# Residual added to the blocks of an output product by accumulating transfers, and their squares queued behind a later weight cast

## The chip, the cores and the metric

The kernel runs on one core of a Trainium2 chip. The metric is device time in microseconds (us) of one execution; lower is better. Before the change it is 2038.79 us, the median of three runs (2037.45 to 2039.75). One execution was profiled, and all durations below come from it.

## The reference, cut to what matters

One layer of a block with 256 rows and a model width of 4096, all in float32:

```python
xn = rms_norm(h, norm_in_g)
q, k, v, z_a, a_c, g_c, z_c = split(xn @ w_in)            # 4096 x 14336
y_a = rms_norm(chunked_attention(q, k, v, rel_table), attn_out_g) * silu(z_a)
y_c = rms_norm(conv_module(a_c, g_c, ...), conv_out_g) * silu(z_c)
h = h + concatenate([y_a, y_c]) @ w_out                    # 4096 x 4096, the changed stage
gate = sigmoid(rms_norm(h, ple_norm_g) @ w_ple_gate + b)   # 4096 x 4096, the stage after it
h = h + gate * (p @ w_ple)
return rms_norm(h, final_g)
```

The change touches the line `h = h + ... @ w_out` (in the first term, `h` is the input `x`) and the sum of squares of its result, which the norm in the next line needs.

## The kernel before, in words

**Products.** Every float32 operand is split into a high part in the fp32r format and a remainder (`parts_of`, L199): ScalarE casts the weight tile `wt` into `wh` (L204), VectorE subtracts to make `wl` (L205). A product of two blocks is three matmuls: high by high, low by high, high by low. There are five `wt` buffers, filled by SyncE's DMAs (L403), and three each of `wh` and `wl`, so a cast waits until TensorE has finished with the tile three before it.

**Groups and pairs.** `mixed_product` (L327) makes one group: 1024 output columns (two column blocks j of 512) for both halves h of the rows, in four PSUM banks `acc[h][j]`. It walks over 16 pairs of contraction blocks. A plain pair takes 24 matmuls. A pair marked with a star takes seven products instead of eight, 21 matmuls, and needs sums of weights, `ua` and `ub`, which VectorE makes (L426 to L431) and which are cast and split too (`uh`, `ul`). Some of the seven go to four helper banks (`P1`, `P5`, `P6`, `P7`). After the group's last starred pair `on_helpers` empties these. The order of the pairs is written by hand: `dense` is "1 0* 3 2* 5 4* 6* 7 8* 9 10* 11 12* 14* 13 15", so two plain pairs follow the last starred one; `late` begins with eight plain pairs.

**The stage of the change** (L1044 to L1073) has four groups of `w_out`. For each, two tiles `hc` (128 partitions, 2 halves, 512 columns) are loaded from `x` (L1049). `on_helpers` (L1054) adds `P1` to the residual in place (L1057), makes three sums of helper banks in a scratch tile `z` (`helper_sums`, L464: a ScalarE copy at L467, four VectorE additions at L468 to L471), and folds these into `hc` with three more VectorE operations (L1059 to L1061). After the last pair VectorE adds the four banks `acc` (L1070), in the order (0,0), (1,0), (0,1), (1,1) of `QUARTERS`. For each quarter a square with a sum over the columns (`square_sum`, L498, run by ScalarE at L500) goes into the queue `later`, from which `fill` (L182) takes two entries after each pair. At the end the queue is emptied, and `rstd_of` (L502) makes the factor `r_h` from the sums (VectorE, then a power on GpSimd at L139).

**The stage after it**, four groups of `w_ple_gate` (L1082 and L1120 to L1164), uses the finished `hc` tiles as its left operand: `h_ahead` (L1037) has TensorE transpose them (L170), ScalarE make the high part (L156) and VectorE the remainder (L157), the first two tiles ahead of the last pair of the last `w_out` group and then one tile ahead of each second pair of the first gate group, whose order is `late` and whose `fill` takes four entries. `r_h` is first used in that group's `on_helpers`.

**Order on the engines.** A scheduler places the instructions at build time, by data and buffer dependences and by when it takes them to be ready. On the chip each engine's queue then runs strictly in that order: an instruction that waits holds everything behind it on its engine.

Of the kernel before, what the change touches and what calls it, by code (L numbers as in the profile page):

```python
# [3 lines left out]

# [6 lines left out]
F32 = mybir.dt.float32  # L11
F32R = mybir.dt.float32r
AF = mybir.ActivationFunctionType
ALU = mybir.AluOpType
AX = mybir.AxisListType

P = 128
NB = 512
# [7 lines left out]
def hybrid_block(  # L26
# [23 lines left out]
    nc = tc.nc  # L50
    _, T, D = x.shape
    NH = T // P
# [15 lines left out]
    def pool(name, bufs, stack=ctx, side=0, **kw):  # L68
        return stack.enter_context(tc.tile_pool(name=name, bufs=bufs, side=sides[side], **kw))

    cpool = pool("cpool", 1)
    act = pool("act", 8)
# [63 lines left out]
    def rsqrt(dst, src, n):  # L136

        nc.vector.tensor_scalar(dst, src, 1.0 / n, EPS, ALU.mult, ALU.add)
        nc.gpsimd.tensor_tensor(dst, dst, mhalf[:, : dst.shape[1]], ALU.pow)  # L139
# [40 lines left out]
    later = deque()  # L180

    def fill(n):  # L182
        for _ in range(min(n, len(later))):
            later.popleft()()


    def weight_parts(w, col, k0, kc, tiles=None):

        wt = wpool.tile([P, KC, NB], F32, tag="w", name="wt")
        nc.sync.dma_start(  # L190
            wt[:, :kc, :],
            w[k0 * P : (k0 + kc) * P, col : col + NB].rearrange("(k q) n -> q k n", q=P),
        )
        return parts_of(wt, kc, tiles)[0]

    def part_tiles():
        return [wpool.tile([P, KC, NB], F32R, tag=tag, name=tag, bufs=3) for tag in ("wh", "wl")]

    def parts_of(wt, kc, tiles=None):  # L199
        if tiles is None:  # L200
            tiles = part_tiles()
        wh, wl = tiles
        made = (
            nc.scalar.copy(wh[:, :kc, :], wt[:, :kc, :]),  # L204
            nc.vector.tensor_tensor(  # L205
                wl[:, :kc, :], wt[:, :kc, :], wh[:, :kc, :].bitcast(F32), ALU.subtract
            ),
        )
        return (wh, wl), made

    def accumulate(acc, h, lhs, kb, wh, wl, k, kblocks, then=lambda ins: None):
        t, i = lhs[kb // 4], kb % 4
        xh = t[:, i, 0, h * P : (h + 1) * P]
        xl = t[:, i, 1, h * P : (h + 1) * P]
        for kind in range(3):
            a, b = ((xh, wh), (xl, wh), (xh, wl))[kind]
            then(
                nc.tensor.matmul(  # L218
                    acc, a, b[:, k, :],
                    start=kb == 0 and kind == 0, stop=kb == kblocks - 1 and kind == 2,  # L220
                )
            )
# [85 lines left out]
    def pair_parts(src):  # L308

        tiles = [upool.tile([P, 2, NB], F32R, tag=tag, name=tag) for tag in ("uh", "ul")]  # L310
        return parts_of(src, 2, tiles)[0]
# [14 lines left out]

    def mixed_product(  # L327
        w, col, lhs, comb, order, on_helpers, ahead=None, fills=(0,), on_begin=None, apart=NB,
        left=(), begin=None,
    ):  # L330
# [64 lines left out]
        for n, (pair, seven) in enumerate(order):  # L395
# [9 lines left out]
            if n >= len(order) - n_left:  # L405
                for k in range(2):
                    tiles = left[2 * (n - len(order) + n_left) + k]
                    held.append((2 * pair + k, parts_of(wts[k], 2, tiles and tiles())[0]))
                fill(fills[n % len(fills)])
                continue  # L410
# [44 lines left out]
            if n == last_seven:  # L455
                on_helpers(helper)
# [4 lines left out]
    tt, stt = nc.vector.tensor_tensor, nc.vector.scalar_tensor_tensor  # L461
    QUARTERS = ((0, 0), (1, 0), (0, 1), (1, 1))

    def helper_sums(helper, z):  # L464


        nc.scalar.copy(z[1][0], helper["P1"])  # L467
        tt(z[1][0], helper["P6"], z[1][0], ALU.add)  # L468
        tt(z[0][1], helper["P5"], z[1][0], ALU.add)
        tt(z[1][0], helper["P7"], z[1][0], ALU.add)  # L470
        tt(z[1][1], helper["P5"], z[1][0], ALU.add)  # L471

    def sum_tiles():

        t = [spool.tile([P, NH, NB], F32, tag="stage", name="z") for _ in range(2)]
        return t, [[t[j][:, h] for j in range(2)] for h in range(NH)]

    def scaled_pair(w, col, apart, order, r, fills, **kw):

        t, z = [], []  # L480

        def on_helpers(helper):
            for dst, src in zip((t, z), sum_tiles()):
                dst.extend(src)
            nc.scalar.activation(z[0][0], helper["P1"], AF.Identity, scale=r[:, :1])
            helper_sums(helper, z)
            for h, j in QUARTERS[1:]:
                nc.scalar.activation(z[h][j], z[h][j], AF.Identity, scale=r[:, h : h + 1])

        c = mixed_product(w, col, xT, xS, order, on_helpers, fills=fills, apart=apart, **kw)  # L490
        for h, j in QUARTERS:
            stt(  # L492
                z[h][j], c[h][j], r[:, h : h + 1], z[h][j],
                ALU.mult, ALU.subtract if j else ALU.add,
            )
        return t

    def square_sum(dst, src, scale=1.0):  # L498
        junk = spool.tile([P, NB], mybir.dt.bfloat16, tag="junk", name="junk", bufs=1)
        return nc.scalar.activation(junk[:, : src.shape[1]], src, AF.Square, scale=scale, accum_out=dst)  # L500

    def rstd_of(partial, n, name):  # L502
        r = cpool.tile([P, partial.shape[1]], F32, name=name)
        nc.vector.tensor_reduce(r, partial, AX.X, ALU.add)
        rsqrt(r, r, n)
        return r
# [433 lines left out]
    for c0, order in zip(range(0, CW // NB, 2), point):  # L940
        row = broadcast_row(b_pw, c0 * NB, 2 * NB, tag="stage")
        rows = [row[:, j * NB : (j + 1) * NB] for j in range(2)]
        ys, z = [], []
# [4 lines left out]
        def on_helpers(helper):  # L948
            y_tiles()
            z.extend([ys[j][:, h, :] for j in range(2)] for h in range(NH))  # L950
            tt(z[0][0], helper["P1"], rows[0], ALU.add)
            helper_sums(helper, z)
            for h, j in QUARTERS[1:]:
                tt(z[h][j], z[h][j], rows[j], ALU.subtract if j else ALU.add)

        acc = mixed_product(w_pw[0], c0 * NB, uS, uC, order, on_helpers)
# [35 lines left out]
    def before_last(make):  # L992

        return lambda pair: make(0) if pair == dense[-1][0] else None
# [29 lines left out]
    hs, hT, hS = [], [], []  # L1024
# [17 lines left out]
                embedding()  # L1042

    ssq_h = cpool.tile([P, NH, D // NB], F32, name="ssq_h")  # L1044
    for c0 in range(0, D // NB, 2):
        for j in range(2):
            hc = act.tile([P, NH, NB], F32, tag="act", name="hc")
            c = c0 + j
            nc.sync.dma_start(  # L1049
                hc, x[0, :, c * NB : (c + 1) * NB].rearrange("(h q) n -> q h n", q=P)  # L1050
            )
            hs.append(hc)

        def on_helpers(helper):  # L1054
            _, z = sum_tiles()
            h00, h01, h10, h11 = (hs[c0 + j][:, h, :] for h in range(NH) for j in range(2))
            tt(h00, helper["P1"], h00, ALU.add)  # L1057
            helper_sums(helper, z)
            tt(h01, h01, z[0][1], ALU.subtract)  # L1059
            tt(h10, h10, z[1][0], ALU.add)  # L1060
            tt(h11, h11, z[1][1], ALU.subtract)  # L1061

        acc = mixed_product(
            w_out[0], c0 * NB, yT, yS, dense if c0 else late, on_helpers,
            ahead=y_ahead if c0 == 0 else before_last(h_ahead) if c0 + 2 == D // NB else None,
            fills=(2,),
        )
        for h, j in QUARTERS:
            hc = hs[c0 + j][:, h, :]
            tt(hc, acc[h][j], hc, ALU.add)  # L1070
            later.append(partial(square_sum, ssq_h[:, h, c0 + j : c0 + j + 1], hc))
    fill(len(later))
    r_h = rstd_of(ssq_h, D, "r_h")  # L1073


    n_f = D // NB
# [47 lines left out]
    c0 = n_f - 2  # L1124
    _, z = sum_tiles()
# [17 lines left out]
    def on_helpers(helper):  # L1143
# [4 lines left out]
    acc, add_left = mixed_product(  # L1148
        w_ple_gate[0], c0 * NB, hT, hS, final, on_helpers, fills=(4,), on_begin=on_begin,
        left=[None] * 3 + [kept] * 3,  # L1150
    )
# [119 lines left out]
```

## Time and profile before

| | us |
|---|---|
| median of 3 runs (lowest, highest) | 2038.79 (2037.45, 2039.75) |
| profiled execution | 2039.1 |
| its span in the profile | 2037.3 |
| TensorE busy in the span | 2019.6 |
| VectorE busy | 1887.9 |
| ScalarE busy | 1200.8 |
| GpSimd busy | 8.1 |
| the four `w_out` groups | about 1329 to 1664 of the span |
| first L1070 of each group | 1415.1, 1496.4, 1578.0, 1661.5 |

How to read it: times inside the execution are microseconds from the start of the span. A matmul's bar in the profile is 0.39 us long, but the next one begins about 0.227 us after it, so the bars overlap and a busy share of TensorE counts gaps only where they are longer than the overlap. "PE" is TensorE, "DVE" VectorE, "ACT" ScalarE, "POOL" GpSimd, "SP" SyncE (a q behind it is its queue).

### The profile page before, as it was taken

To read this page: it belongs to the slowest core of one execution; us is meant where nothing else is said; L and a number is where in the kernel's file an instruction comes from. 1 tells how busy PE (TensorE), PEld (TensorE's weight loads), DVE (VectorE), ACT (ScalarE), POOL (GpSimd) and SP (SyncE) were. 2 spreads that over 40 slices of the span, in tenths; PEclk is the share of its full clock that TensorE was granted. 3 is DMA by queue.
4 is the path that set the end of the run, shared out by engine and by line. 5 is a ranking of instruction groups with operands and counts; after the bars stand their busy time and mean duration, and the time that the engine had idled before them with its cause. 6 is when DMAs were issued, how large, how long until landed. Compare 5 with 4: busy or idle time off the path is not lost.

```text
span 2037.3 us, 26041 instructions
## 1 busy us (share of the span) xinstructions
PE 2019.6 (99%) x9106; PEld 1659.5 (81%) x9106; DVE 1887.9 (93%) x2688; ACT 1200.8 (59%) x1559; POOL 8.1 (0%) x19
## 2 busy tenths in 40 slices
PE   9999999999999999999999999999999999999997
PEld 7888888877888888888888888888888888888876
DVE  7999999799989998868899999999999999999998
ACT  7655546554565546676555656676565666655555
POOL 0000000000000000000000000000000000000000
PEclk9999999999999999999999999999999999999999
DMA  8666665666656665655666666676666656666765
GB/s 295 188 200 204 204 187 165 202 191 189 184 185 204 201 188 183 186 184 199 190 216 204 197 216 199 219 238 204 214 201 205 214 185 208 198 221 205 235 208 179
DMA packets 161853, 412.29 MB, mean 202 GB/s; under 512 B 12974, under 2 KB 16190, under 8 KB 161722
## 3 DMA queue, kind: packets, MB, share of 16 engines
q1 hardware_dynamic: 161072, 409.80, 63.3%
q8 instruction: 71, 1.16, 0.2%
q10 hardware_dynamic: 650, 0.84, 0.1%
q14 instruction: 60, 0.49, 0.1%
HBM read 406.39 MB, written 4.19 MB: 202 GB/s over the span
## 4 chain that ended last, share of the span: by engine, by line
PE 86%; DVE 10%; issue 2%; DMA 1%; ACT 1%; POOLq 0%; POOL 0%; ACTq 0%; DVEq 0%
PE acc L370 61%; PE acc_P L370 15%; PE acc L218 7%; DVE wl L205 4%; DVE cv L677 3%; DMA wt<-in_w_in_dram 1%; PE tmp_ps L170 1%; DVE ul L205 1%; PE tmp_ps L867 0%; PE tmp_ps L849 0%; ACT wh L204 0%; PE acc L358 0%; PE tmp_ps L834 0%; DVE z L492 0%; PE tmp_ps L872 0%
## 5 line engine op out<-in xcount | busy, mean ns | idle before, releaser
L370 PE MATMUL acc<-wh,big_t 128*128 128x512 f32 x3788 | 1172.1, 391 | 0.6 <-DVE z L988 0.3
L204 ACT CAST wh<-wt 128x1024 fp32r<-128x1024 f32 (+1 forms) x737 | 715.8, 982 | 543.0 <-PE acc L370 330.6
L205 DVE TENSOR_TENSOR wl<-wt,wh 128x1024 fp32r<-128x1024 f32 (+1 forms) x737 | 825.4, 1132 | 65.0 <-ACT wh L204 60.1
L370 PEld LDWEIGHTS acc<-wh,big_t 128*128 128x128 f32 x3788 | 708.4, 188 | 146.5 <-issue 0.6
L370 PE MATMUL acc<-wl,big_t 128*128 128x512 f32 x1894 | 731.1, 391 | 1.0 <-DVE wl L205 1.0
L370 PEld LDWEIGHTS acc<-wl,big_t 128*128 128x128 f32 x1894 | 355.2, 188 | 76.7 <-DVE wl L205 3.1
L677 DVE SCALAR_TENSOR_TENSOR cv<-uT,dw,cv 128x255 f32<-128x255 f32 (+23 forms) x480 | 204.9, 467 | 1.1
L204 ACT CAST uh<-ub 128x1024 fp32r<-128x1024 f32 x122 | 128.5, 1054 | 126.2 <-DVE ub L431 102.7
L218 PE MATMUL acc<-wh,big_t 128*128 128x512 f32 x560 | 173.1, 390 | 0.0
L204 ACT CAST uh<-ua 128x1024 fp32r<-128x1024 f32 x122 | 128.7, 1055 | 71.7 <-DVE ua L427 63.5
L205 DVE TENSOR_TENSOR ul<-ub,uh 128x1024 fp32r<-128x1024 f32 x122 | 149.0, 1221 | 8.8 <-ACT uh L204 7.8
L370 PE MATMUL acc_P<-uh,big_t 128*128 128x512 f32 x504 | 154.4, 392 | 0.0
L205 DVE TENSOR_TENSOR ul<-ua,uh 128x1024 fp32r<-128x1024 f32 x122 | 148.9, 1220 | 0.4 <-ACT uh L204 0.2
L218 PEld LDWEIGHTS acc<-wh,big_t 128*128 128x128 f32 x560 | 104.8, 188 | 21.4
L370 PEld LDWEIGHTS acc_P<-uh,big_t 128*128 128x128 f32 x504 | 93.3, 188 | 22.2 <-ACT uh L204 3.7
L218 PE MATMUL acc<-wl,big_t 128*128 128x512 f32 x280 | 109.1, 390 | 0.0
L426 DVE TENSOR_TENSOR ua<-wt 128x512 f32<-128x512 f32 x122 | 83.9, 688 | 25.9 <-DMA wt<-in_w_in_dram 19.0
L370 PE MATMUL acc_P<-ul,big_t 128*128 128x512 f32 x252 | 96.8, 392 | 0.0
L427 DVE TENSOR_TENSOR ua<-wt 128x512 f32<-128x512 f32 x122 | 83.7, 686 | 3.9 <-DMA wt<-in_w_in_dram 3.0
L431 DVE TENSOR_TENSOR ub<-ub,wt 128x512 f32<-128x512 f32 x122 | 83.8, 687 | 1.0
L430 DVE TENSOR_TENSOR ub<-ua,wt 128x512 f32<-128x512 f32 x122 | 83.7, 686 | 0.3
L370 PE MATMUL acc<-uh,big_t 128*128 128x512 f32 x244 | 75.4, 390 | 0.0
(241 smaller groups left out, 1523.0 us busy)
## 6 DMA issues: line engine op xcount, KB each, us to landing
wt<-in_w_in_dram SPq DMA_DIRECT2D x447, 512.0 KB, 4.0
wt<-in_w_out_dram SPq DMA_DIRECT2D x128, 512.0 KB, 4.2
wt<-in_w_ple_gate_dram SPq DMA_DIRECT2D x128, 512.0 KB, 4.2
wt<-in_w_pw_dram SPq DMA_DIRECT2D x32, 512.0 KB, 4.5
hc<-in_x_dram SPq DMA_DIRECT2D x8, 512.0 KB, 5.8
wt<-in_w_ple_dram SPq DMA_DIRECT2D x8, 512.0 KB, 4.2
xin<-in_x_dram SPq DMA_DIRECT2D x7, 512.0 KB, 8.2
out_dram<-hc SPq DMA_DIRECT2D x12, 256.0 KB, 2.4
```

The lines of the kernel that those rows point to most:

```text
L170: nc.tensor.transpose(pt[:, i * T + h * P : i * T + (h + 1) * P], src[:, h, b * P : (b + 1) * P], ident,)
L204: nc.scalar.copy(wh[:, :kc, :], wt[:, :kc, :]),
L205: nc.vector.tensor_tensor(wl[:, :kc, :], wt[:, :kc, :], wh[:, :kc, :].bitcast(F32), ALU.subtract),
L218: nc.tensor.matmul(acc, a, b[:, k, :], start=kb == 0 and kind == 0, stop=kb == kblocks - 1 and kind == 2,)
L370: nc.tensor.matmul(banks[name], a, b, start=name not in begun, stop=final and ends[name] == n and kind == 2 and not (left and name in "P2 ...
L426: plus(ua[:, 0], w0[:, 0], w0[:, 1])
L427: plus(ua[:, 1], w0[:, 1], w1[:, 1])
L430: plus(ub[:, 0], ua[:, 0], w1[:, 1])
L431: plus(ub[:, 1], ub[:, 0], w1[:, 0])
L677: nc.vector.scalar_tensor_tensor(cv[:, i, PAD - k :], uT[:, i, : T + k - PAD], dw[:, b, k : k + 1], cv[:, i, PAD - k :], ALU.mult, ALU.add,)
```

## The change

Each group's two `hc` tiles are no longer loaded before the product. `on_helpers` writes the helper sums straight into them: ScalarE copies `P1` into the quarter (0,0), and `helper_sums` makes the other three there. After the last pair VectorE adds or subtracts the four banks in place, as before four operations. Then GpSimd issues for each tile a DMA that adds the block of `x` to what lies in the tile (`accum_op`). The squares wait for these transfers. They are put into the queue four entries later than before (four empty entries ahead of them), and `square_later` orders each behind the ScalarE cast of the most recently split weight, without waiting for that cast's end. `r_h` is no longer made by emptying the queue at the end of the stage but as an entry of the queue, eight empty entries behind the last squares, within the first gate group.

As it is built, TensorE's queue has the same instructions as before, in the same order but for some matmuls and transposes at the passage from the last `w_out` group to the first gate group. SyncE's queue loses the eight loads of `x`, GpSimd's gains eight DMAs between the powers of `r_c` and `r_h`, and VectorE's loses L1057 and L1059 to L1061 of each group.

```diff
@@ parts_of
+        recent[:] = made
         return (wh, wl), made
+
+    recent = []
+
+    @contextmanager
+    def queued_behind(made):
+
+        with ExitStack() as queued:
+            for ins in made:
+                queued.enter_context(tc.issue_after(ins.ins))
+            yield
@@
     ssq_h = cpool.tile([P, NH, D // NB], F32, name="ssq_h")
+    def square_later(dst, src):
+        with queued_behind(recent[:1]):
+            square_sum(dst, src)
+
+    def x_columns(c):
+        return x[0, :, c * NB : (c + 1) * NB].rearrange("(h q) n -> q h n", q=P)
+
     for c0 in range(0, D // NB, 2):
-        for j in range(2):
-            hc = act.tile([P, NH, NB], F32, tag="act", name="hc")
-            c = c0 + j
-            nc.sync.dma_start(
-                hc, x[0, :, c * NB : (c + 1) * NB].rearrange("(h q) n -> q h n", q=P)
-            )
-            hs.append(hc)
+        hs.extend(act.tile([P, NH, NB], F32, tag="act", name="hc") for _ in range(2))
+        z = [[hs[c0 + j][:, h, :] for j in range(2)] for h in range(NH)]
 
         def on_helpers(helper):
-            _, z = sum_tiles()
-            h00, h01, h10, h11 = (hs[c0 + j][:, h, :] for h in range(NH) for j in range(2))
-            tt(h00, helper["P1"], h00, ALU.add)
+            nc.scalar.copy(z[0][0], helper["P1"])
             helper_sums(helper, z)
-            tt(h01, h01, z[0][1], ALU.subtract)
-            tt(h10, h10, z[1][0], ALU.add)
-            tt(h11, h11, z[1][1], ALU.subtract)
@@
         for h, j in QUARTERS:
-            hc = hs[c0 + j][:, h, :]
-            tt(hc, acc[h][j], hc, ALU.add)
-            later.append(partial(square_sum, ssq_h[:, h, c0 + j : c0 + j + 1], hc))
-    fill(len(later))
-    r_h = rstd_of(ssq_h, D, "r_h")
+            tt(z[h][j], acc[h][j], z[h][j], ALU.subtract if j else ALU.add)
+        for j in range(2):
+            nc.gpsimd.dma_start(hs[c0 + j], x_columns(c0 + j), accum_op=ALU.add)
+        later.extend([lambda: None] * 4)
+        for h, j in QUARTERS:
+            later.append(partial(square_later, ssq_h[:, h, c0 + j : c0 + j + 1], z[h][j]))
+    r_h = cpool.tile([P, NH], F32, name="r_h")
+
+    def scale_h():
+        nc.vector.tensor_reduce(r_h, ssq_h, AX.X, ALU.add)
+        rsqrt(r_h, r_h, D)
+
+    later.extend([lambda: None] * 8 + [scale_h])
```

More of the change, by code (lines that the diff above doesn't have):

```diff
@@ L1 @@
 from collections import deque
-from contextlib import ExitStack
+from contextlib import ExitStack, contextmanager
 from functools import partial
```

## The prediction

> **What bounds the kernel now.** First the page: the span, TensorE's busy row, and the chain of work that ended last.
>
> ```profile
> span 2037.3 us, 26041 instructions
> PE 2019.6 (99%) x9106; PEld 1659.5 (81%) x9106; DVE 1887.9 (93%) x2688; ACT 1200.8 (59%) x1559; POOL 8.1 (0%) x19
> PE 86%; DVE 10%; issue 2%; DMA 1%; ACT 1%; POOLq 0%; POOL 0%; ACTq 0%; DVEq 0%
> ```
>
> VectorE, at 93%, looks like a near second, and the change takes work off it. But these shares are means over the run. So I read the changed stage alone, in stretches of 85 us (columns: length, busy time of each engine, clock, DMA share), and then the chain there: first by line over 1300 to 1720, then three of its pieces with start, length and count.
>
> ```profile
> 1325.00:1410.00 85.00, 85.00 (x398) 70.12 (x397) 81.76 (x132) 56.05 (x81) 0.00 (x0) 1.00 0.69 226
> 1495.00:1580.00 85.00, 85.00 (x377) 70.32 (x376) 81.50 (x99) 52.01 (x62) 0.00 (x0) 1.00 0.64 208
> 1580.00:1665.00 85.00, 85.00 (x388) 70.66 (x387) 81.46 (x106) 53.11 (x69) 0.00 (x0) 1.00 0.60 200
> 1665.00:1750.00 85.00, 85.00 (x399) 70.74 (x398) 80.84 (x126) 55.21 (x84) 0.69 (x1) 1.00 0.63 202
> by line: PE acc L370 76.5%; PE acc_P L370 20.2%; PE tmp_ps L170 3.4%
> 1358.16 5.49 PE acc L370 x24
> 1432.32 2.04 PE acc_P L370 x9
> 1486.72 17.00 PE acc L370 x75
> ```
>
> From 1325 to 1750 TensorE is busy in every microsecond and the chain holds nothing but TensorE. Bars overlap, so the pieces are the sharper test: 17.00/75 and 2.04/9 both give 0.227 us a matmul, the same pace in long and short pieces; the slowest plain pair, in the first group, takes 5.49 instead of 24 x 0.2267 = 5.44. So the stage runs at TensorE's pace. VectorE's 96% there is no bound: it only has to stay ahead. With 0.05 us lost per plain pair in the first group, all that a faster VectorE could give back is below 1 us.
>
> **What the change removes and adds.** The rows of the lines concerned (count, then ns least/median/most; the last two are all of their line, not the change's alone):
>
> ```profile
> L1057 DVE TENSOR_TENSOR hc<-acc_P,hc x4: 682/683/692, 1402.7 to 1646.7; 128x512 f32<-128x512 f32 x4
> L1059 DVE TENSOR_TENSOR hc<-hc,z x4: 681/682/682, 1408.7 to 1653.1; 128x512 f32<-128x512 f32 x4
> L1060 DVE TENSOR_TENSOR hc<-hc,z x4: 681/682/682, 1409.9 to 1654.3; 128x512 f32<-128x512 f32 x4
> L1061 DVE TENSOR_TENSOR hc<-hc,z x4: 685/685/686, 1410.5 to 1654.9; 128x512 f32<-128x512 f32 x4
> L1070 DVE TENSOR_TENSOR hc<-acc,hc x16: 681/683/692, 1415.1 to 1666.6; 128x512 f32<-128x512 f32 x16
> L467 ACT COPY z<-acc_P x20: 568/575/589, 84.4 to 1996.6; 128x512 f32<-128x512 f32 x20
> L500 ACT ACTIVATE junk<-hc x33: 417/632/640, 1415.9 to 2026.9; 128x512 bf16<-128x512 f32 x31, 128x256 bf16<-128x256 f32 x2
> SPq L1049 <- PE tmp_ps L170: 14.9, 7, 6.6
> ```
>
> VectorE loses 16 operations, 16 x 0.683 = 10.9 us; L1070 stays at 16. ScalarE gains 4 copies, 4 x 0.575 = 2.3 us. On the time both count as nothing: TensorE covers them, and ScalarE is busy 50 to 56 of 85 us. If that cover went, the 10.9 us would be the most to gain. SyncE loses eight loads and the 14.9 us in which they waited for a tile and held the weight loads behind them; those loads start earlier, which also falls into the stretch at 85.00 of 85 and gives nothing.
>
> **The new waits.** The moved step is the add of `x`: eight DMAs of 512 KB from GpSimd's queue, each after the second (or fourth) L1070 of its group, and the squares wait for them in ScalarE's queue, ahead of casts. No accumulating DMA and none issued by GpSimd is in this trace, so its price must be bounded. The nearest rows: the time that the weight queue's packets took, landings of weights, landings of the same `x` blocks (least/median/most), and GpSimd's power for `r_h`.
>
> ```profile
> q1 hardware_dynamic: 161072, 409.80, 63.3%
> wt<-in_w_out_dram SPq DMA_DIRECT2D x128, 512.0 KB, 4.2
> DMA to landing us min/median/max: 3.7/5.8/6.7
> 1669.02 0.69 POOL L139 TENSOR_TENSOR r_h<-r_h,mhalf 128x2 f32<-128x2 f32 x1 [667.58 <-DVE r_h L138]
> ```
>
> 409.80 MB are 782 times 512 KB, and 63.3% of 2037.3 us spread over them is 1.65 us of all engines for each. From below: 3.7 us, the fastest load of the same block. From above: the slowest, 6.7 us, twice, 13.4 us, if adding doubles everything. I take 4.2 + 1.65 + 0.69 = 6.5 us: a weight's landing, once more the engine time because the old contents must be read too, and one short GpSimd operation for the issue. It lies nearest to the loads of `x`, and at the passage that matters the engines are empty (below).
>
> A rule of the Trainium skill speaks for the second read and against the change: "Collectives: The Full Stack", section "The bandwidth ceiling: the fold count and why AG ≠ RS ≠ AR", says that a transfer that adds needs two source reads through one queue, and gives 32.35 against 62.28 GB/s. By its ratio of 1.93 the second read would cost 0.93 x 1.65 = 1.5 us, an estimate that moves the sum by 0.1 us. No run here shows it yet.
>
> **Passages between `w_out` groups (three).** ScalarE and VectorE around the first of them:
>
> ```profile
> 1423.83 1.04 ACT L204 CAST wh<-wt 128x1024 fp32r<-128x1024 f32 x1
> 1425.37 0.62 ACT L204 CAST wh<-wt 128x512 fp32r<-128x512 f32 x1 [0.49 <-ACT wh L204]
> 1415.14 2.48 DVE L1070 TENSOR_TENSOR hc<-acc,hc 128x512 f32<-128x512 f32 x4
> ```
>
> The first tile is complete after two of the four L1070, at 1416.4. In the built order the first squares stand behind the second cast of the next group's third pair, here the one that ends at 1424.9; so the transfer has 8.5 us before ScalarE notices, more than 6.5. If ScalarE is held, what hangs behind is the half-tile cast for pair 2, whose products begin at 1432.3: take off two squares with their reads (1.65), the cast (0.62) and about 0.7 for VectorE's remainder, and TensorE is hit only if the transfer lands after 1429.3, 12.9 us after the start. The second tile's squares come one pair later. Cost 0; at the upper bound about 0.5 us each.
>
> **The last passage, into the first gate group.** Here the slack is small: ScalarE also makes the operands of the next product, and `fill` takes four entries, so that the squares come after two pairs, not three. VectorE, ScalarE, TensorE, and the DMA share (last but one column) there:
>
> ```profile
> 1661.51 0.68 DVE L1070 TENSOR_TENSOR hc<-acc,hc 128x512 f32<-128x512 f32 x1
> 1664.37 1.28 DVE L1070 TENSOR_TENSOR hc<-acc,hc 128x512 f32<-128x512 f32 x2
> 1670.37 0.88 DVE L157 SCALAR_TENSOR_TENSOR big_t<-tmp_ps,prm,big_t 128x256 fp32r<-128x256 f32 x2
> 1671.15 1.22 DVE L205 TENSOR_TENSOR wl<-wt,wh 128x1024 fp32r<-128x1024 f32 x1
> 1668.21 1.06 ACT L204 CAST wh<-wt 128x1024 fp32r<-128x1024 f32 x1
> 1669.18 0.83 ACT L156 ACTIVATE big_t<-tmp_ps,prm 128x256 fp32r<-128x256 f32 x2
> 1672.55 0.62 PE L370 MATMUL acc<-wh,big_t 128*128 128x512 f32 x2
> 1673.00 0.39 PE L370 MATMUL acc<-wl,big_t 128*128 128x512 f32 x1
> 1664.00:1666.00 2.00, 2.00 (x16) 1.78 (x16) 1.70 (x5) 1.49 (x4) 0.00 (x0) 1.00 0.03 8
> 1666.00:1668.00 2.00, 2.00 (x10) 1.65 (x9) 2.00 (x3) 1.97 (x6) 0.00 (x0) 1.00 0.00 0
> ```
>
> In the changed ScalarE queue the first square stands right behind the cast that was at 1668.21, ahead of the two L156 that were at 1669.18. VectorE's two L157 (1670.37) need these L156, and behind them, in order, is the remainder `wl` (1671.15, ready 1672.37) that TensorE wants at 1673.00. So a late square holds ScalarE, then VectorE, then TensorE. Backwards from 1673.00: `wl` 1.22, the L157 behind the second L156 0.47, two L156 0.83, the square with its read 0.8: it must start by 1669.7. The tile is complete after the second L1070, about 1664.8 (VectorE has hardly a gap from 1657 on, so the operations removed at 1655 bring nothing forward). The transfer has 1669.7 - 1664.8 = 4.9 us and takes 6.5: **TensorE waits 1.6 us**. At the lower bound nothing, at the upper 8.5.
>
> The second tile, complete about 1666.3, lands by 1666.3 + 6.5 + 1.8 for the rest of the first one's two reads = 1674.6. Behind its squares stands the cast for the second half of the third pair (products from about 1678.5), which may begin at 1676.5: no more cost. On GpSimd nothing stands behind the transfers but the power for `r_h`. `r_h` is first used ten pairs later, and the transposes of these two tiles come in the sixth and seventh pair, over 25 us on: nothing.
>
> **Sum.** 2037.3 of span and 1.8 around it are the profiled 2039.1, 0.3 above the median of the runs. With 1.6 it is **2040.7**. 0.2%, about what a measurement of this kernel can tell from no change, is 4.1 us: below 2034.7 is faster, above 2042.9 slower.
>
> **Rivals.**
> 1. Hidden: the transfer lands within 4.9 us. For it: the empty DMA engines and the 3.7 us row. Against: the median of 5.8 for the plain load. Time 2038 to 2039.6, the same. Chance 0.20.
> 2. Slower by slow accumulation: a landing over 8.9 us holds ScalarE's in-order queue at the last passage by more than 4 us. The deciding point is that landing; the place is the first square behind the cast of 1668.21. At 13.4 us: 8.5 there, 0.5 at each of three other passages, 2039.1 + 10 = 2049. For it: weights are loaded again from 1668 on, at 0.8 of the engines, and share with the second tile. Chance 0.22.
> 3. Slower because GpSimd cannot write its descriptors while VectorE runs without gaps: if the issue waits behind three VectorE operations of 1.22 us, the landing is 10.2, the wait 5.3, the time 2044.4. Against it: the `r_h` row, where GpSimd reads and writes SBUF in 0.69 us amid a gapless VectorE. Chance 0.09. The Trainium skill has this rule in "SBUF — State Buffer", section "SBUF: two separate sides": VectorE operations in a two-port mode lock GpSimd out and starve its DMAs. By that rule the `r_h` row agrees that the operations of this stage don't lock.
> 4. Faster, or not what it says: TensorE's pace hides a loss that goes with VectorE's 10.9 us. The chain speaks against it: at most 1 us, to 2038. Chance 0.05, of which 0.03 below 2034.7 for what I don't see.
>
> **How the numbers follow.** Forecast (a wait of 0.5 to 4 us at the last passage, 2039.6 to 2042.9) 0.44. Slower is rivals 2 and 3, 0.31; the same is the forecast, rival 1 and the rest of 4, 0.66; faster 0.03. The range goes from 2037.5 (the lowest run before) to 2047: it leaves out the upper half of rival 2 and the faster cases, about 0.15.
>
> **What would show it.** Right: TensorE's only new wait lies at about 1673, behind VectorE's L157 and a ScalarE square that waits for a DMA; transfers land in 6 to 7 us; L1057 and L1059 to L1061 are gone; busy 85.00 of 85 before that. Wrong: TensorE waits at passages between `w_out` groups (then landings exceed 12.9 us), a long GpSimd issue (rival 3), or a shorter pace of the matmuls (rival 4).

## The result and the profile after

| | us |
|---|---|
| before, median of 4 runs beside the changed kernel (lowest, highest) | 2038.92 (2037.45, 2039.75) |
| after, median of 4 runs (lowest, highest) | 2056.84 (2053.72, 2057.99) |
| ratio after to before, 95% interval | 1.0085 (1.0072 to 1.0098) |
| profiled execution after, its span | 2053.72, 2051.9 |

The change makes the kernel 17.9 us slower; 2040.7 was forecast, with a range of 2037.5 to 2047. The profiled execution is the fastest of the four. The lines of the page after that answer to those of before:

```profile
span 2051.9 us, 26029 instructions
...
PE 2023.2 (99%) x9106; PEld 1658.7 (81%) x9106; DVE 1878.8 (92%) x2672; ACT 1200.3 (58%) x1563; POOL 18.0 (1%) x27
...
q0 software_dynamic: 2176, 4.19, 1.3%
...
PE 80%; DVE 12%; DMA 3%; issue 3%; ACT 1%; POOLq 0%; POOL 0%; ACTq 0%; DVEq 0%
...
hc<-in_x_dram POOLq DMA_DIRECT2D x8, 512.0 KB, 6.3
```

VectorE lost its 9 us, the transfers land in 6.3 us (6.5 was forecast), and yet TensorE's share of the chain fell from 86% to 80%. Where it waits shows in the stretches of 85 us (length, busy time of TensorE, its weight loads, VectorE, ScalarE, GpSimd, clock, DMA share, GB/s) of the kernel after:

```profile
1325.00:1410.00 85.00, 85.00 (x400) 70.61 (x399) 80.71 (x127) 56.15 (x81) 0.00 (x0) 1.00 0.57 186
1410.00:1495.00 85.00, 82.25 (x359) 66.81 (x358) 75.34 (x89) 48.47 (x59) 2.61 (x2) 1.00 0.66 210
1495.00:1580.00 85.00, 83.22 (x363) 67.39 (x362) 76.74 (x90) 49.32 (x59) 2.44 (x2) 1.00 0.65 211
1580.00:1665.00 85.00, 82.91 (x369) 68.02 (x368) 75.25 (x88) 49.71 (x59) 2.44 (x2) 1.00 0.67 211
1665.00:1750.00 85.00, 80.15 (x381) 65.73 (x380) 75.57 (x130) 55.54 (x93) 3.15 (x3) 1.00 0.63 190
```

All four stretches with a passage lose, 11.5 us of 340 together; the stretch ahead of the first transfer is whole. (Bars of matmuls overlap, so shorter losses come on top.) The waits of the kernel after between 1300 and 1800 (engine and line, what it waited for: total, times, longest):

```profile
DVE ua L437 <- DMA wt<-in_w_out_dram: 21.2, 16, 3.5
...
ACT junk L511 <- DMA hc<-in_x_dram: 7.3, 2, 4.9
...
PE acc L381 <- DVE wl L205: 5.9, 5, 2.1
...
PE tmp_ps L170 <- DMA pin<-in_p_dram: 2.4, 1, 2.4
```

In the kernel before, this view has no row in which TensorE's matmuls wait. The squares (L511, L500 before) hold ScalarE twice, both times at the last passage, 7.3 us together; that was looked for. The first row was not: VectorE waits 21.2 us for *weights*, where the same wait in the kernel before was

```profile
DVE ua L426 <- DMA wt<-in_w_out_dram: 4.9, 9, 1.5
```

and TensorE then waits for the remainders `wl` that stand behind in VectorE's queue. (Run 1 will show that the length of this wait alone is no measure of the loss.) VectorE after at the first passage:

```profile
1414.70 2.48 DVE L1077 TENSOR_TENSOR hc<-acc,hc 128x512 f32<-128x512 f32 x4
1417.09 1.82 DVE L205 TENSOR_TENSOR wl<-wt,wh 128x1024 fp32r<-128x1024 f32 x2
1418.83 1.22 DVE L205 TENSOR_TENSOR ul<-ub,uh 128x1024 fp32r<-128x1024 f32 x1
1419.96 1.22 DVE L205 TENSOR_TENSOR wl<-wt,wh 128x1024 fp32r<-128x1024 f32 x1
1424.68 0.69 DVE L437 TENSOR_TENSOR ua<-wt 128x512 f32<-128x512 f32 x1 [3.50 <-DMA wt<-in_w_out_dram]
```

The remainders at 1417 and 1420 free weight buffers, so three loads start there, beside the transfer that the last additions (1414.70) let go. GpSimd's row shows that transfer, and that the second one comes 6.4 us after it, though its tile was complete 1.2 us later; the bracket is the idle time ahead of it:

```profile
1416.30 1.37 POOL L1079 DMA_DIRECT2D hc<-in_x_dram  x1 [415.99 <-DVE hc L1077]
1422.67 1.24 POOL L1079 DMA_DIRECT2D hc<-in_x_dram  x1 [5.00 <-issue]
...
1673.31 1.21 POOL L1079 DMA_DIRECT2D hc<-in_x_dram  x1 [80.15 <-DVE comb L271]
1679.53 1.22 POOL L1079 DMA_DIRECT2D hc<-in_x_dram  x1 [5.01 <-issue]
```

### The profile page after: what moved, and what is told of

It is laid out like the page before. It is cut to its first block, busy times and chain, and to the rows that moved or that the text cites. A ratio compares the mean times of both kernels' runs of the same rounds, so it can differ in the third digit from the quotient of the medians.

```text
span 2051.9 us, 26029 instructions
## 1 busy us (share of the span) xinstructions
PE 2023.2 (99%) x9106; PEld 1658.7 (81%) x9106; DVE 1878.8 (92%) x2672; ACT 1200.3 (58%) x1563; POOL 18.0 (1%) x27
## 4 chain that ended last, share of the span: by engine, by line
PE 80%; DVE 12%; DMA 3%; issue 3%; ACT 1%; POOLq 0%; POOL 0%; ACTq 0%; DVEq 0%
PE acc L381 56%; PE acc_P L381 14%; PE acc L229 7%; DVE wl L205 5%; DVE cv L688 3%; DMA wt<-in_w_out_dram 2%; DVE ul L205 1%; PE tmp_ps L170 1%; ACT wh L204 1%; DMA hc<-in_x_dram 0%; DMA wt<-in_w_in_dram 0%; DVE ua L438 0%; PE tmp_ps L860 0%; PE tmp_ps L878 0%; DVE big_t L157 0%
## 5 line engine op out<-in xcount | busy, mean ns | idle before, releaser
L437 DVE TENSOR_TENSOR ua<-wt 128x512 f32<-128x512 f32 x122 | 83.8, 687 | 41.5 <-DMA wt<-in_w_out_dram 21.2
```

Of the source, the lines that this page charges most:

```text
L437: plus(ua[:, 0], w0[:, 0], w0[:, 1])
```

## The experiments

Two theories were set against each other. **A**: the transfers take the DMA engines from weight loads that are just in time, VectorE waits for them in order, and TensorE waits for VectorE. **B**: the forecast's mechanism, only larger: squares that wait for a transfer hold ScalarE. A third, **C**, is that the new order of the queues does it without any transfer. Every ratio below is to the kernel before, run beside it; its interval is 95%. Where two runs are compared with each other, the difference of their ratios is uncertain by up to some 0.2%, 4 us (an estimate from the intervals). Code cuts are marked with `...`.

### 1. No transfers

```diff
-        for j in range(2):
-            nc.gpsimd.dma_start(hs[c0 + j], x_columns(c0 + j), accum_op=ALU.add)
```

> The changed kernel without its eight adding transfers: the residual is left out of the sum, everything else stands in the same order on every engine, and the squares wait for nothing but their tile. Theory A (the transfers take the DMA engines from the weights, and the second of a group begins only when the first has drained): all of the loss goes, 2037 to 2041 us, TensorE without gaps from 1325 to 1750. Theory B (forecast's mechanism alone, squares that wait hold ScalarE): the same time, since the waits go too. Theory C (the moved squares, the copy of P1 and the later r_h do the harm): 2048 or more, with VectorE and ScalarE late at the same four passages.

Measured 2040.9 us, ratio 1.0012 (1.0003 to 1.0022). The transfers and what waits for them make 0.73% of the 0.85%; 0.12%, 2.4 us, is there without them, so C holds in small. VectorE waits long for weights without any transfer, too. Between 1300 and 1800, where the kernel after had 21.2 us, this run has

```profile
DVE ua L437 <- DMA wt<-in_w_out_dram: 12.9, 15, 1.9
```

So about half of that row's growth over the 4.9 us of before comes without transfers, with VectorE's new order (run 11 takes it back); what a wait costs TensorE has to be read from the runs. VectorE in this run at the second passage:

```profile
1496.44 0.68 DVE L441 TENSOR_TENSOR ub<-ua,wt 128x512 f32<-128x512 f32 x1
1497.16 0.69 DVE L442 TENSOR_TENSOR ub<-ub,wt 128x512 f32<-128x512 f32 x1
1497.77 1.22 DVE L205 TENSOR_TENSOR wl<-wt,wh 128x1024 fp32r<-128x1024 f32 x1
1498.90 1.22 DVE L205 TENSOR_TENSOR ul<-ua,uh 128x1024 fp32r<-128x1024 f32 x1
1500.04 2.48 DVE L1077 TENSOR_TENSOR hc<-acc,hc 128x512 f32<-128x512 f32 x4
```

In the kernel before, the four last additions came right after the first `ub` (L430); here the second `ub`, a `wl` and a `ul` have been placed ahead of them. The additions free the four banks that the next group needs, and TensorE waits for one of them once, 1.3 us. Runs 5 and 11 take this up.

### 2. Room for two transfers' descriptors

```diff
-dynamic_dma_scratch_size=1024
+dynamic_dma_scratch_size=2048
```

> The changed kernel with twice the room for GpSimd's descriptors (2048 instead of 1024 bytes), the order on all engines the same. If the 6.2 us between the two transfers of a group come from that room, the second issue follows 1.3 us behind the first, and the second tile lands 8 to 10 us after the first issue instead of 12.5. Theory A: the same bytes in a shorter time, so the weights at the passages between w_out groups are as late as before or later (2 to 3.5 us each), and only the last passage gets 3 to 5 us back: 2048 to 2053. Theory B: with the second squares no longer waiting, 2042 to 2046. If the gap between the issues stays at 6.2 us, the room is not its cause and the time stays at 2054 to 2058.

Measured 2052.55 us, 1.0070 (1.0055 to 1.0085). GpSimd's row at the first passage:

```profile
1415.54 2.62 POOL L1079 DMA_DIRECT2D hc<-in_x_dram  x2 [415.54 <-DVE hc L1077]
```

The second issue now follows at once (x2 in one row): the 6.2 us between the issues came from that room, and not from VectorE. About 4 us come back by the medians (3 by the ratios, whose intervals overlap), as A had it; B's 2042 to 2046 is missed.

### 3. Transfers that overwrite instead of adding

```diff
-            nc.gpsimd.dma_start(hs[c0 + j], x_columns(c0 + j), accum_op=ALU.add)
+            nc.gpsimd.dma_start(hs[c0 + j], x_columns(c0 + j))
```

> The changed kernel with transfers that overwrite instead of adding (the product is lost from the result; same bytes written, same queue, same order): the price of the second read. Theory A: packets take about 90 to 110 ns instead of 178, the transfers land in 4 to 5 us, the weights' delay halves: 2045 to 2050. Theory B: the first landing is earlier by 2 us, the second too, but its issue stays behind the first: 2048 to 2054, all of the gain in the last passage.

Measured 2052.18 us, 1.0064 (1.0049 to 1.0079): slower than A had it, and in B's range. The DMA rows of the same 20 us, 1414 to 1434 (queue, packets, MB, share of the 16 engines; then weight loads and transfers with their median landing), first of this run, then of the kernel after:

```profile
q0 software_dynamic: 288, 1.05, 16.0%
...
wt<-in_w_out_dram SPq DMA_DIRECT2D x6, 512.0 KB, 5.6
hc<-in_x_dram POOLq DMA_DIRECT2D x2, 512.0 KB, 6.3
```

```profile
q0 software_dynamic: 544, 1.05, 31.6%
...
wt<-in_w_out_dram SPq DMA_DIRECT2D x7, 512.0 KB, 6.0
hc<-in_x_dram POOLq DMA_DIRECT2D x2, 512.0 KB, 7.1
```

Adding doubles the engine time: 31.6% of 20 us for two transfers are 3.2 us each, 16.0% are 1.6 us. By these rows a packet takes 178 ns here and 186 after, where 90 to 110 was expected; there are half as many (288 instead of 544). The weights do not gain from it: VectorE's longest row of waits for them is 24.9 us (21.2 after). Issuing a plain transfer takes 0.72 us of GpSimd instead of 1.21, the second follows within 0.8 us, and both then fall on the same loads. At the last passage, where the squares waited only 0.7 us, TensorE lost nothing (85.00 of 85), so the gain lies where B put it; but the three passages before it lose 8.2 us, at which B has nothing.

### 4. A transfer for the first tile alone

```diff
-        for j in range(2):
+        for j in range(1):
             nc.gpsimd.dma_start(hs[c0 + j], x_columns(c0 + j), accum_op=ALU.add)
```

> The changed kernel with an adding transfer for the first tile of each group only (x is not added to the second): half the bytes and nothing to queue behind. Theory A with the load on the DMA engines in proportion to bytes: about half of the 15 to 18 us goes at the first three passages, and more than half at the last: 2043 to 2047. Theory A with the queueing of the second transfer as the whole harm: 2039 to 2041. Theory B: only the first square of the last passage waits (2.4 us in the changed kernel's trace): 2040 to 2043, TensorE whole at the first three passages.

Measured 2049.75 us, 1.0056 (1.0041 to 1.0071), slower than any theory had it. The loads that start in the 7 us after the first passage's last additions, here and in the kernel after (1416 to 1423.5) and before (1418 to 1423), three each:

```profile
wt<-in_w_out_dram SPq DMA_DIRECT2D x3, 512.0 KB, 6.7
```

```profile
wt<-in_w_out_dram SPq DMA_DIRECT2D x3, 512.0 KB, 6.3
```

```profile
wt<-in_w_out_dram SPq DMA_DIRECT2D x3, 512.0 KB, 4.1
```

The first tile's transfer alone delays these three as much as both do. The harm is not in proportion to bytes: one transfer beside these loads is enough. At the last passage the first square waited 2.6 us and TensorE 1.5 us, close to the 1.6 us of the forecast.

### 5. The moved squares alone, on the kernel before

```diff
...
-            later.append(partial(square_sum, ssq_h[:, h, c0 + j : c0 + j + 1], hc))
-    fill(len(later))
-    r_h = rstd_of(ssq_h, D, "r_h")
+        sq = []
...
+            sq.append(partial(square_later, ssq_h[:, h, c0 + j : c0 + j + 1], hc))
+        later.extend([lambda: None] * 4 + sq)
...
+    later.extend([lambda: None] * 8 + [scale_h])
```

> The kernel before with one part of the change alone: the squares queued two pairs into the next group behind a cast, and r_h made as an entry of the queue. The residual is loaded by SyncE and added by VectorE as before, and there is no transfer by GpSimd. The changed kernel without its transfers still lost 2.3 us (2040.9), with VectorE's last additions behind more of the next group's weight work. If the moved squares and r_h do that, the time is 2040 to 2042 here too; if it is the 16 VectorE operations taken away (the scheduler fills their place with the next group's work), the time is that of before, 2037.5 to 2039.5. Theory B says nothing of it: no transfer, no wait.

Measured 2039.09 us, 0.9998 (0.9989 to 1.0008): the moved squares and `r_h` cost nothing. So the 2.4 us of run 1 belong to the VectorE operations that were taken away.

### 6. The transfers held back

```diff
...
+        def send(c0=c0, hold=c0 + 2 < D // NB):
+            for j in range(2):
+                ins = nc.gpsimd.dma_start(hs[c0 + j], x_columns(c0 + j), accum_op=ALU.add)
+                if hold:
+                    tc.add_manual_dep(ins.ins, recent[1].ins.name, ...)
+        if c0 + 2 < D // NB:
+            later.extend([lambda: None] * 5 + [send] + [lambda: None] * 8)
+        else:
+            send()
+            later.extend([lambda: None] * 4)
```

> The changed kernel with the transfers of the first three groups held back: GpSimd waits for a remainder of about the third pair of the next group, some 8 to 12 us later than the last additions, and the squares come later by as much. The last group is left alone. Theory A, sharpened (what hurts is that the transfer starts together with the three weight loads that the last additions let go, which land in 6.3 to 6.9 us instead of 3.7 to 5): those loads land in 3.7 to 5 us again, the first three passages cost no more than without transfers (about 2 us together), 2046 to 2051 in all. If any place in the stage is as bad, because the weights are just in time everywhere, 2054 to 2059, with three late loads where the transfers now lie. Theory B: squares never waited at these passages, so nothing changes: 2055 to 2058.

Measured 2057.99 us, 1.0090 (1.0073 to 1.0107): nothing is won. The loads beside the last additions (1414 to 1422) are in time again, and two that now have the second transfer beside them (1435.5 to 1441) are late:

```profile
wt<-in_w_out_dram SPq DMA_DIRECT2D x3, 512.0 KB, 3.8
```

```profile
wt<-in_w_out_dram SPq DMA_DIRECT2D x2, 512.0 KB, 5.4
```

So the sharpened form of A is wrong in its place: the collision was real, but the weights are just in time at the new place as well, and TensorE waits 7.5 us for `wl`. B had the same time, and no reason for these waits. (At most 3.4 us are of another kind: the clock granted to TensorE is 0.98 in two stretches here; see run 8.)

### 7. Squares that read another tile

```diff
+    ones = cpool.tile([P, NB], mybir.dt.bfloat16, name="ones")
+    nc.vector.memset(ones, 1.0)
...
-            later.append(partial(square_later, ssq_h[:, h, c0 + j : c0 + j + 1], z[h][j]))
+            later.append(partial(square_later, ssq_h[:, h, c0 + j : c0 + j + 1], ones))
```

> The changed kernel with its transfers, but the squares read a constant tile (their sums are left out), so that no square waits for a transfer; only the transposes of the first gate group still do, far later. Theory A: the first three passages lose as much as before (about 7 us of gaps); the last passage, where ScalarE was held 2.4 and 4.9 us, is whole but for late weights: 2048 to 2052. Theory B: no held ScalarE, no loss: 2039 to 2043.

Measured 2048.64 us, 1.0041 (1.0026 to 1.0056). This divides the loss: 0.44%, 9.0 us, goes with the held squares, and 0.29%, 5.9 us, is left above run 1 for what the transfers do otherwise, which A puts on the late weights. The third and the fourth passage of this run, then the loads of the first gate group that start in 1680 to 1687:

```profile
1580.00:1665.00 85.00, 81.50 (x362) 66.57 (x361) 74.39 (x86) 48.96 (x58) 2.44 (x2) 1.00 0.66 211
1665.00:1750.00 85.00, 85.00 (x407) 70.82 (x405) 81.60 (x135) 59.53 (x98) 3.15 (x3) 1.00 0.67 209
```

```profile
wt<-in_w_ple_gate_dram SPq DMA_DIRECT2D x4, 512.0 KB, 8.2
```

At the last passage four loads land in 8.2 us, later than the 6.3 us at the first passage of the kernel after, and TensorE loses nothing. That group begins with eight plain pairs. So a late weight need not cost. That it depends on which pair the weight belongs to is a guess here, and the ground for run 9.

### 8. The transfers ahead of the last additions

The two calls stand at the end of `on_helpers`, with room for 2048 bytes. (In the columns of j = 1 the last operation subtracts the tile, so the residual comes out with the wrong sign there.)

> The changed kernel with the transfers moved up to right behind the helper sums, about 10 us ahead of the last additions, and room for both transfers' descriptors (2048 bytes). The last additions now wait for the transfers, the squares no longer. Theory A: the transfer meets the weight loads of the last two pairs instead of the next group's first, which are as much just in time; and where a transfer lands after the end of the group (over 10 us), VectorE is held: 2045 to 2055, no ScalarE wait at the last passage. If the collision with the next group's first loads is all: 2040 to 2043. Theory B: 2040 to 2042, as long as the landing stays below 10 us.

Measured 2059.41 us, 1.0093 (1.0078 to 1.0108), above every expectation. Its waits between 1300 and 1800:

```profile
DVE hc L1079 <- DMA hc<-in_x_dram: 16.3, 8, 2.7
PE acc L381 <- DVE hc L1079: 12.2, 6, 2.7
```

The transfers take 9.1 us, the last additions wait for them, and TensorE waits for the banks. At the first passage the issue began at 1408.85 and VectorE came to the additions at 1413.74: 4.9 us, not the 10 that were expected. So the run shows that 4.9 us are too few, and not that a place still earlier would cost as much; VectorE's waits for weights (both `ua` lines) are 11.6 us here against 22.4 in the kernel after. Part of the time is of another kind. The clock granted to TensorE, 1.00 in every stretch shown of the kernels before and after, is 0.98, 0.96 and 0.96 (last but two column) in the three stretches from 1410 to 1665:

```profile
1495.00:1580.00 85.00, 80.50 (x344) 65.69 (x343) 73.28 (x85) 48.41 (x57) 2.46 (x2) 0.96 0.63 199
```

The missing 0.02, 0.04 and 0.04 of 85 us each make 8.5 us; that is the most that the clock can have cost (an estimate). In this run and in run 6 the low clock lies behind gaps of 2.1 to 2.7 us in TensorE; behind the gap of 2.4 us in the kernel after it did not come, so what sets it off is not shown.

### 9 and 10. Another order of pairs, after and before

```diff
+    spread = units("1 0* 3 5 2* 4* 7 6* 8* 9 10* 11 12* 14* 13 15")
...
-            w_out[0], c0 * NB, yT, yS, dense if c0 else late, on_helpers,
+            w_out[0], c0 * NB, yT, yS, spread if c0 else late, on_helpers,
```

> The changed kernel with the pairs of the second to fourth w_out group in another order, 1 0* 3 5 2* 4* 7 6* 8* 9 10* 11 12* 14* 13 15: the weights that arrive with the transfers (the loads of the fourth pair and of the first tile of the fifth) now belong to a plain pair, 5, and to 2* behind it, where they were those of 2* and 5. Theory A, sharpened (a late weight costs only where VectorE, whose queue is in order, needs it for the sums ua of a starred pair; in the first gate group, which begins with plain pairs, loads of 8 us cost TensorE nothing): the gaps at the three passages go for the most part, 2049 to 2053. If late weights cost the same in a plain pair, 2055 to 2059. Nothing is done about the last passage and its 8 us. Theory B: no difference at these passages, 2055 to 2058.

> Control: the kernel before with the same other order of pairs. If that order costs or gives nothing by itself: 2038 to 2040. If VectorE falls behind in it (two starred pairs in a row come more often), 2040 to 2045, and what the other run shows has to be read against this one.

The changed kernel: 2048.3 us, 1.0048 (1.0033 to 1.0062). The control: 2037.78 us, 0.9999 (0.9990 to 1.0009). An order that is worth nothing to the kernel before gives the changed one 0.37%, 7.5 us, a little more than A had it. Its waits between 1300 and 1800:

```profile
DVE ua L438 <- DMA wt<-in_w_out_dram: 17.0, 12, 4.0
...
DVE ua L439 <- DMA wt<-in_w_out_dram: 3.6, 4, 1.3
PE acc L382 <- DVE wl L205: 2.9, 5, 1.2
```

The weights are as late as before (17.0 + 3.6 against 21.2 + 1.2 us for the two `ua` lines), but TensorE's waits for `wl` are halved, 2.9 instead of 5.9. With a plain pair there, VectorE has finished more of the next pairs' operands before it comes to the late sum. That reading fits, but only the order was tried, not the reason. Part of the 7.5 us lies at the last passage (1.9 us of the stretch 1665 to 1750), on which the order should have no bearing.

### 11. No transfers, and the last additions tied ahead

```diff
...
+            with ExitStack() as queued:
+                if n == 1 and last_add:
+                    queued.enter_context(tc.issue_after(last_add.pop().ins))
+                uah, ual = pair_parts(ua)
+                w1h, w1l = parts_of(w1, 2)[0]
+                plus(ub[:, 0], ua[:, 0], w1[:, 1])
...
-            tt(z[h][j], acc[h][j], z[h][j], ALU.subtract if j else ALU.add)
+            last_add[:] = [tt(z[h][j], acc[h][j], z[h][j], ALU.subtract if j else ALU.add)]
```

> The changed kernel without its transfers (the residual is left out), and the sums ub and remainders of each group's first starred pair tied behind the last additions of the group before, as they lay in the kernel before. If the 2.3 us that are lost without transfers come from VectorE's last additions, which free TensorE's banks, standing behind the next group's sums: 2037.5 to 2039.5. If they come from the weights' timing (VectorE reaches the sums sooner and waits there): 2040 to 2042, as without the tie.

Measured 2038.32 us, 1.0001 (0.9992 to 1.0010), with 85.00 of 85 in all stretches, and VectorE's waits for weights at 6.4 us (both `ua` lines; 16.0 in run 1). The 2.4 us of run 1 were the order: with 16 operations gone, the scheduler had filled their place with the next group's work, ahead of the additions that free the banks.

### 12. Three cures together

Runs 9 and 11's edits on the changed kernel, and for the last group `[lambda: None] * 12` instead of 4 ahead of the squares.

> The changed kernel with three cures together: the other order of pairs, the last additions ahead of the next group's sums, and the last group's squares eight queue entries (two pairs) later, when both transfers have landed. All of the residual is added. If the three causes found are all there are (2 us of order, 8 of late weights, 8 of held squares): 2038 to 2042, at best the time of before, since TensorE has no gap left to give. If the order of pairs does not help: 2046 to 2050. Theory B (held squares alone): 2039 to 2041 too, but with the gaps at the first three passages cured by nothing but the squares, which did not wait there.

Measured 2044.43 us, 1.0032 (1.0020 to 1.0043): a gain, but not what three causes would leave. ScalarE in this run:

```profile
1433.68 0.63 ACT L515 ACTIVATE junk<-hc 128x512 bf16<-128x512 f32 x1 [1.88 <-DMA hc<-in_x_dram]
...
1517.02 0.63 ACT L515 ACTIVATE junk<-hc 128x512 bf16<-128x512 f32 x1 [3.23 <-DMA hc<-in_x_dram]
...
1602.13 0.63 ACT L515 ACTIVATE junk<-hc 128x512 bf16<-128x512 f32 x1 [4.78 <-DMA hc<-in_x_dram]
```

Now the squares of the second tile hold ScalarE at the other three passages too. Two things moved. Counted from the first issue, ScalarE comes to these squares 1.4 to 2.2 us sooner than in the changed kernel, and the second issue comes 7.5 to 8.1 us behind the first instead of 6.0 to 6.4. Why GpSimd's wait grew is not shown.

### 13 and 14. All squares later, without and with the room

Run 12 with `[lambda: None] * 12` for every group; run 14 with 2048 bytes besides.

> The run with the three cures, and the squares of all groups eight queue entries later, not only the last group's. In the run with the three cures ScalarE still waited at the passages between w_out groups for the second transfer, up to 4.8 us, since its issue came 6 to 8 us behind the first. If held squares are what was left of the 6.6 us: 2037.5 to 2040, no gap over 0.6 us in TensorE from 1300 to 1800. If late weights still cost, whatever the order of pairs: 2042 to 2045, with VectorE's waits for weights ahead of the gaps. It is not expected below the time of before: TensorE has no gap there to give.

> The same with room for both transfers' descriptors (2048 bytes). The second issue follows 1.3 us behind the first, so that both transfers fall on the same weight loads. If the weights' lateness is what counts now, this is slower than the run without that room, by 1 to 3 us; if nothing waits any more, the two are the same within 1 us.

Run 13: 2038.5 us, 1.0004 (0.9995 to 1.0014). Run 14: 2039.82 us, 1.0013 (1.0005 to 1.0022). The stretches of run 13:

```profile
1410.00:1495.00 85.00, 85.00 (x375) 70.01 (x375) 77.95 (x92) 51.33 (x61) 2.61 (x2) 1.00 0.70 217
1495.00:1580.00 85.00, 85.00 (x375) 70.05 (x375) 79.18 (x93) 49.87 (x60) 3.06 (x3) 1.00 0.68 218
1580.00:1665.00 85.00, 85.00 (x389) 70.67 (x389) 79.19 (x103) 54.36 (x71) 2.98 (x3) 1.00 0.65 209
1665.00:1750.00 85.00, 85.00 (x398) 70.68 (x397) 80.71 (x124) 55.02 (x85) 1.98 (x3) 1.00 0.70 219
```

With the eight adding transfers and the whole residual, TensorE is without a gap again, in the time of the kernel before. So cures for the order of work, the late weights and the held squares are together enough to take the whole loss away. What is not separated is which cure made the late weights harmless. VectorE's waits for weights (both `ua` lines) were 20.6 us in run 9 and fall to 8.8 in run 12 and 10.3 in run 13, which also tie the additions; no run ties them and keeps the old order of pairs. None of these versions is faster than before: TensorE had nothing left to give. The room for both transfers, worth 3 to 4 us in run 2, costs 1.3 us here by the medians and 0.09% by the ratios, whose intervals overlap. That VectorE waits longer for weights then, 14.4 instead of 10.3 us, would fit a cost; that there is one is not shown.

## Why the prediction was wrong, by its own steps

- **What bounds the kernel** (TensorE; VectorE "only has to stay ahead"): right. No run was measurably faster than before, whatever it took off VectorE.
- **The removed VectorE work counts as nothing**: no gain, as forecast, but a loss of 2.4 us by the order that the scheduler made of the gap (runs 1, 5, 11; a price without transfers, since in the changed kernel itself TensorE waits only 0.5 us for a bank). The order was looked at on TensorE, SyncE and GpSimd, and on ScalarE for the squares; that of VectorE's last additions against the next group's weights was passed over.
- **SyncE's eight loads**: nothing, right (run 13 has the time of before without them).
- **The transfer, 6.5 us**: 6.3 in the median (5.7 to 8.1), right, and in part by luck: the issue was set at 0.69 us and takes 1.21 to 1.37, and the rest is shorter by about as much. The second read is 1.6 us more of all engines, as taken. The Trainium skill, in "Collectives: The Full Stack", section "The bandwidth ceiling: the fold count and why AG ≠ RS ≠ AR", says of ReduceScatter that its add needs two source reads; the trace of this transfer agrees, 3.2 against 1.6 us of all engines, a ratio of 1.98 where the page's figures give 1.93.
- **Passages between `w_out` groups, "Cost 0"**: this is the step that failed. What it asked, whether the transfer lands before its squares, was answered rightly: no square waited there in the changed kernel. But the transfer was charged for its own landing alone. What it does to the weight loads beside it was put at nothing without a word, though the waits of before showed VectorE already waiting for weights (4.9 us, nine times). In its place the runs showed loads of 4.1 us that land in 6.3 and TensorE waiting behind VectorE at all three passages; price 5.9 us (run 7 less run 1, where no square waits). The prediction's sign of being wrong named this place, but with landings above 12.9 us; the longest was 8.1. "DMA: Bandwidth & Descriptors" in the Trainium skill, section "Issuing engines are not separate DMA queues", says that transfers run on the same 16 engines and interleave whichever engine started them; the trace agrees with the first passage's loads, and the prediction thought of sharing only at the last passage.
- **The last passage, 1.6 us**: the mechanism was right and mis-sized. For the first tile it was close: ScalarE held 2.4 us and TensorE 1.3 (2.6 and 1.5 in run 4). For the second tile the prediction had a landing at 1674.6 and "no more cost", taking both transfers as issued together. The second issue came 6.2 us later and its square held ScalarE 4.9 us, as it landed 14.1 us after the first issue, where the prediction had 9.8. TensorE waited 0.7 and 0.5 us behind that, and 2.4 us for the tile of `p`, whose load SyncE issued at 1718.9 instead of 1704.5 (before); without held squares (run 7) none of these waits is there. Together 9.0 us (after less run 7).
- **Rivals**: the second (held squares, about 2049) named the place of the largest part, but the adding was not slow, the second transfer was late. The third (VectorE keeps GpSimd from writing descriptors) is out: the wait between the issues goes with the room alone (run 2). No rival had late weights.

The sum by the ratios: 2.4 + 5.9 + 9.0 = 17.3 us, 0.85% of 2039. It closes by construction, since each term is the difference between two runs of one chain (before, 1, 7, after), and the last two are uncertain by some 4 us each. The check from outside is run 13, which treats all three causes, adds the whole residual, and has the time of before.

## What to carry to other kernels

A transfer that is added beside just-in-time loads must be charged for their delay, not only for its own landing: look in the waits of *before* whether any engine already waits for those loads. A mean DMA share of 0.64 was no slack here, where five buffers are refilled one by one. And an operation taken away becomes a new order of work, as in run 1: look where the operations that free someone else's buffers come to stand.

## What the runs showed of the hardware

- A second adding transfer of 512 KB from GpSimd waited about 5 us, mostly for nothing that the profile names, while the room for descriptors was 1024 bytes, and followed within 0.4 us with 2048 (runs after and 2). A plain one was not held at 1024 (run 3).
- Issuing an adding transfer takes GpSimd 1.21 to 1.37 us, a plain one of the same size 0.72 to 0.87 (runs after and 3).
- A transfer beside three weight loads took them from 4.1 to 6.3 us; one transfer was as bad as two (6.7, run 4), and at the last passage four loads took 8.2 us at no cost to TensorE (run 7).
- An adding transfer took twice the packets of a plain one and twice the engine time (544 against 288, 3.2 against 1.6 us; runs after and 3).
